# The last feed-forward by seven block products instead of eight, in rounds of three, and the linear attention of the same kernel in another order

## The chip, the cores and the metric

The kernel runs on one core of a Trainium2 chip as a single program. The metric is the time of one execution on the device in microseconds (us). Three executions of the kernel before gave 2459.79, 2460.69 and 2461.81 us; the median is 2460.69 us. One further execution was recorded by the profiler and took 2456.27 us; everything that is read from a trace below is from that one.

The core has a matrix engine (PE, with its weight loads shown apart as PEld), a vector engine (DVE), a scalar engine (ACT), a general engine (POOL) and an engine that mostly issues transfers (SP). Each runs its own queue of instructions in order.

## What is computed

One inference step of a two-layer decoder trunk for 544 tokens: 512 of a prompt and 8 short sequences of 4 tokens. Layer 0 mixes tokens with gated linear attention, layer 1 with a forgetting attention. Before and after each mixer stands a feed-forward, so there are four.

```python
def swiglu(u, w_up, w_down):
    a, b = jnp.split(u @ w_up, 2, axis=-1)
    return (jax.nn.silu(a) * b) @ w_down

def gla_mixer(u, s0, w_in, w_gate2, b_gate, g_out, w_out):
    ...
    q, k, v, r, glr = jnp.split(u @ w_in, [dk, 2 * dk, 2 * dk + dv, 2 * dk + 2 * dv], axis=-1)
    log_a = jax.nn.log_sigmoid((glr @ w_gate2 + b_gate).astype(jnp.float32)) / GLA_TAU
    ...
    o, S = gla_chunk_scan(q * GLA_DK ** -0.5, k, v, log_a, s0)
    o = rmsnorm(o, g_out).reshape(B, L, dv).astype(u.dtype) * jax.nn.silu(r)
    return o @ w_out, S.astype(s0.dtype)

u = modulate(h, P['g_norm'][layer, 2], mod[:, 2, 0], mod[:, 2, 1])
h = h + 0.5 * mod[:, 2, 2][:, None, :] * swiglu(u, P['w_ffn_up'][layer, 1], P['w_ffn_down'][layer, 1])
```

The model width is 1024, the feed-forward's inner width 2816, so `w_up` is 1024 x 5632 (gate columns first, then value columns) and `w_down` 2816 x 1024. The linear attention has 4 heads with keys of 128 and values of 256. Everything is in 32-bit floats.

## The kernel before

**Numbers in two halves.** Every large product is made of three matmuls: an operand x is split into a rounded part (`...h`, written by ACT as a cast) and the rest (`...l`, DVE: x minus the rounded part), and the helper `acc3` adds hi·hi, hi·lo and lo·hi into a PSUM bank (L176 to L178). `halves` (L156) makes the two parts of anything; `split` and `split_cols` (L160, L168) load weights with a transfer and then call it. Weights pass through `raw_tile` (4 buffers), `hi_tile` and `lo_tile` (6 each). PSUM banks for products come from `mm_bank` (5 of them), small ones from `aux_bank` (2).

**Layout.** The 544 columns of tokens stand in two halves of 272, features in 8 blocks of 128 on the partitions (`uh`, `ul` are the input of a feed-forward in two parts, `h` is the residual stream).

**Feed-forward** (`ffn`). The 2816 inner features make 22 pairs of 128 gate and 128 value columns. `up(q, half)` is a gate product `pa` and a value product `pb`, 8 blocks x 3 matmuls each; ACT takes Silu from `pa`, DVE multiplies by `pb` (L446), and `halves` makes `gh`, `gl`. So a pair has 96 up matmuls. `down(qs)` takes a round of pairs (2, then five times 4), loads their rows of `w_down` (128 x 1024 each, one piece) and makes 16 blocks (8 feature blocks x 2 halves) `pd`, each with 3 matmuls per pair of the round. `residual` adds a block into `h`: a DVE operation on the prompt's columns (L393), and in the second half a small DVE product `gs` (L396) and a POOL addition (L398) for the samples. The ups of the next pairs stand behind the 16 blocks of a round. After the last round, `store` transposes `h` and writes the result.

**Linear attention** (`gla`). In order: queries q0 to q3 (`gq`), the third piece of the values with the 16 gate columns (`gv2`), transposes of the gates, then all 8 gate products `z` (L731; contraction over 16 rows), Abs (ACT) and min (DVE) on each; Exp and Ln over all heads (L734, L735), and on DVE per head a subtraction (L737) and a scan (L738), which gives the decay sums `bb`. The other values `gv0`, `gv1` follow (`proj_tokens`), which covers that chain on PE. Then a loop over 4 heads and 7 levels (64 down to 1): DVE (L794) and POOL or DVE (L795) write differences of `bb` to one of four `xb` buffers, ACT takes Exp (L796), DVE and POOL multiply by q and k (L797, L798), PE makes the products of the level (L806), and DVE copies them out (L809, L811). Between the levels `fill` puts projections that don't depend on it on PE: keys k0 to k3 and receptances r0 to r7; the list `FL` says how many after which level. Behind the loop come the samples' part (`ats`, L822 to L842), then per head (L852 to L859) two Exp into a tile `ex`, a product on DVE, a difference on DVE and a product on POOL, which leave q and k ready for the loop over chunks (L899 on), whose transposes `pk` come first.

## Time and profile before

| what | value |
|---|---|
| median of three executions | 2460.69 us (2459.79 to 2461.81) |
| the profiled execution | 2456.27 us |
| its span, first to last instruction | 2454.2 us (2.07 us lie around it) |
| PE busy | 2391.9 us, 97% |
| DVE, ACT, POOL busy | 1236.1, 782.0 and 289.6 us (50, 32 and 12%) |
| mean granted PE clock | 0.986 |
| bytes moved | 319.38 MB, mean 130 GB/s |

A share of the whole span is a mean over stages; the table by stage is shown in the prediction. Matmuls overlap in the records (one of 272 columns lasts 0.29 us while the next starts 0.125 us later), so PE's work is counted by how many start in a full stretch, not by the sum of durations.

### The profile page before, as it was taken

How to read it: one execution, taken by the hardware profiler on the slowest of the kernel's cores; microseconds unless marked ns; L12 is line 12 of the kernel's file. 1: busy time of each engine (PE TensorE's matmuls, PEld its weight loads, DVE VectorE, ACT ScalarE, POOL GpSimd, SP SyncE). 2: the span in 40 equal slices, each digit the busy share in tenths (PEclk: the TensorE clock that was granted, in tenths of full speed). 3: DMA queues.
4: the chain of work that ended last, by engine and by line, in shares of the span. 5: the costliest groups of instructions: out<-in, count | busy, mean ns of one | idle time of the engine just before them, and what ended most of it. 6: DMA issues, size and time to landing. Idle time of an engine off the chain costs nothing.

```text
span 2454.2 us, 48240 instructions
## 1 busy us (share of the span) xinstructions
PE 2391.9 (97%) x20204; PEld 2244.3 (91%) x20204; DVE 1236.1 (50%) x2823; ACT 782.0 (32%) x1430; POOL 289.6 (12%) x448
## 2 busy tenths in 40 slices
PE   8999999999899999999999999999998899999999
PEld 6999999998879999999989999999895589999999
DVE  6343334547666344444584444434848656444433
ACT  4222222334534212222335222222347444222221
POOL 0000000204302010000220000001325120000000
PEclk8999999989999999999999999999999899999999
DMA  9637444313171646445357322322148642222221
GB/s 304 215 115 234 154 167 154 91 48 96 36 223 57 226 141 223 160 167 169 117 152 220 102 86 76 104 87 70 57 104 204 168 125 78 87 92 90 72 84 55
DMA packets 325519, 319.38 MB, mean 130 GB/s; under 512 B 24607, under 2 KB 276349, under 8 KB 325254
## 3 DMA queue, kind: packets, MB, share of 16 engines
q1 hardware_dynamic: 311526, 304.43, 39.0%
q0 software_dynamic: 13776, 11.87, 2.3%
q8 instruction: 159, 2.61, 0.4%
q14 instruction: 58, 0.48, 0.1%
HBM read 298.17 MB, written 18.38 MB: 129 GB/s over the span
## 4 chain that ended last, share of the span: by engine, by line
PE 86%; DVE 5%; DMA 4%; ACT 2%; POOL 1%; issue 1%; SPq 0%; ACTq 0%; DVEq 0%; POOLq 0%
PE pa L176 7%; PE pb L178 7%; PE pb L177 7%; PE pa L177 7%; PE pa L178 7%; PE pb L176 7%; PE pd L176 7%; PE pd L178 7%; PE pd L177 7%; PE ada L231 3%; DMA kd<-khscr 1%; PE kv L588 1%; PE kv L587 1%; PE kv L589 1%; DVE nv L367 1%
## 5 line engine op out<-in xcount | busy, mean ns | idle before, releaser
L176 PE MATMUL pa<-uh,hua 128*128 128x272 f32 x1408 | 410.4, 291 | 1.9 <-ACT uh L386 1.8
L177 PE MATMUL pa<-ul,hua 128*128 128x272 f32 x1408 | 408.6, 290 | 0.4 <-DVE ul L387 0.2
L178 PE MATMUL pb<-uh,lub 128*128 128x272 f32 x1408 | 407.9, 290 | 0.0
L178 PE MATMUL pa<-uh,lua 128*128 128x272 f32 x1408 | 407.6, 289 | 0.0
L176 PE MATMUL pd<-gh,hwd 128*128 128x272 f32 x1408 | 406.8, 289 | 0.0
L176 PE MATMUL pb<-uh,hub 128*128 128x272 f32 x1408 | 406.1, 288 | 0.0
L177 PE MATMUL pb<-ul,hub 128*128 128x272 f32 x1408 | 406.1, 288 | 0.0
L178 PE MATMUL pd<-gh,lwd 128*128 128x272 f32 x1408 | 405.3, 288 | 0.0
L177 PE MATMUL pd<-gl,hwd 128*128 128x272 f32 x1408 | 405.1, 288 | 0.0
L393 DVE SCALAR_TENSOR_TENSOR h<-pd,mods,h 128x272 f32<-128x272 f32 (+1 forms) x384 | 185.2, 483 | 250.8 <-PE pd L178 249.8
L176 PEld LDWEIGHTS pa<-uh,hua 128*128 128x128 f32 x1408 | 266.2, 189 | 14.7 <-issue 6.0
L177 PEld LDWEIGHTS pa<-ul,hua 128*128 128x128 f32 x1408 | 266.4, 189 | 1.6 <-DVE ul L387 1.6
L177 PEld LDWEIGHTS pb<-ul,hub 128*128 128x128 f32 x1408 | 266.7, 189 | 0.0
L176 PEld LDWEIGHTS pd<-gh,hwd 128*128 128x128 f32 x1408 | 265.2, 188 | 1.7 <-issue 1.6
L176 PEld LDWEIGHTS pb<-uh,hub 128*128 128x128 f32 x1408 | 266.4, 189 | 0.0
L178 PEld LDWEIGHTS pb<-uh,lub 128*128 128x128 f32 x1408 | 266.4, 189 | 0.0
L178 PEld LDWEIGHTS pa<-uh,lua 128*128 128x128 f32 x1408 | 266.3, 189 | 0.0
L177 PEld LDWEIGHTS pd<-gl,hwd 128*128 128x128 f32 x1408 | 265.5, 189 | 0.0
L178 PEld LDWEIGHTS pd<-gh,lwd 128*128 128x128 f32 x1408 | 265.4, 188 | 0.0
L446 DVE TENSOR_TENSOR g<-g,pb 128x272 f32<-128x272 f32 x176 | 77.1, 438 | 350.3 <-PE pb L178 348.9
L157 ACT CAST hua<-rua 128x1024 fp32r<-128x1024 f32 x88 | 92.2, 1048 | 461.4 <-PE pd L177 349.6
L398 POOL TENSOR_TENSOR h<-h,gs 128x32 f32<-128x32 f32 x192 | 70.8, 369 | 1237.5 <-DVE gs L396 1232.0
(497 smaller groups left out, 4167.1 us busy)
## 6 DMA issues: line engine op xcount, KB each, us to landing
adaw<-in_w_ada_dram SPq DMA_DIRECT2D x128, 512.0 KB, 6.1
rua<-in_w_ffn_up_dram SPq DMA_DIRECT2D x88, 512.0 KB, 3.8
rub<-in_w_ffn_up_dram SPq DMA_DIRECT2D x88, 512.0 KB, 3.9
rwd<-in_w_ffn_down_dram SPq DMA_DIRECT2D x88, 512.0 KB, 5.0
adah<-in_w_ada_dram SPq DMA_DIRECT2D x16, 512.0 KB, 7.8
adaw<-in_w_ada_kv_dram SPq DMA_DIRECT2D x16, 512.0 KB, 7.5
s<-in_state_gla_dram SPq DMA_DIRECT2D x16, 512.0 KB, 4.2
kp<-in_cache_k_dram SPq DMA_DIRECT2D x16, 512.0 KB, 4.5
```

Of the source, the lines that this page charges most:

```text
L157: S.copy(hi, src)
L176: PE.matmul(ps, lhsT=wh, rhs=xh, start=first and i == 0, stop=False)
L177: PE.matmul(ps, lhsT=wh, rhs=xl, start=False, stop=False)
L178: PE.matmul(ps, lhsT=wl, rhs=xh, start=False, stop=last and i == n - 1)
L231: PE.matmul(ps[32 * j:32 * j + 32, 0:256], lhsT=sc[:, k, :], rhs=t[:, j * 256:(j + 1) * 256], start=k == 0, stop=k == NB - 1)
L367: V.scalar_tensor_tensor(out=v[:, 0:p1 - t0], in0=h[:, k, t0:p1], scalar=mods[:, scale + k, 0:1], in1=rb[:, t0:p1], op0=ALU.mult, op1=ALU. ...
L393: V.scalar_tensor_tensor(out=h[:, m, t0:p1], in0=ps[:, 0:n], scalar=mods[:, gate + m, 0:1], in1=h[:, m, t0:p1], op0=ALU.mult, op1=ALU.add)
L398: G.tensor_tensor(out=h[:, m, TP:T], in0=h[:, m, TP:T], in1=st[:], op=ALU.add)
L446: V.tensor_tensor(out=g[:], in0=g[:], in1=pb[:, 0:HA], op=ALU.mult)
L587: PE.matmul(o, lhsT=xh, rhs=wh, start=k == 0, stop=False)
L588: PE.matmul(o, lhsT=xh, rhs=wl, start=False, stop=False)
L589: PE.matmul(o, lhsT=xl, rhs=wh, start=False, stop=k == NB - 1)
```

## The change

**In the last feed-forward** the call of `ffn` is replaced by a new function `ffn_seven`. Pairs 0 to 2 are computed as before. For the other 19 pairs the up product is regarded as a product of 2 x 2 blocks (gate and value columns by lower and upper 512 rows of the weights, times lower and upper 512 features by the two token halves), and is made with 7 block products, where the plain way has 8. A block product is 4 blocks x 3 matmuls on 272 columns. The sums that this takes: four of the inputs, T1 to T4, once (`inputs`, DVE, 11 operations of 128 x 272 for each of 4 blocks, and `last_input`); four of each pair's weights on POOL (`stage` 0 and 1, 128 x 512 each), whose halves ACT and DVE make in `stage` 1 to 4; and seven per pair with which DVE takes the products out of PSUM (`plus_ps`). The first product goes out by an ACT copy. The lower part `gl` is made by POOL (`low`), in the last round by DVE. Down rounds have 3 pairs (six of them) and 2 (two), and the 16 blocks of a round are put between the 7 products of each pair of the next round (`between`). The rows of `w_down` come as four pieces of 256 columns per round.

**In the linear attention** the projections start as q0, k0, q1, k1, then `gv2`. The gate products `z` stand between the steps of `gv0`; the gate sums of head 0 follow, those of heads 1 to 3 stand behind levels 1, 3 and 5 of head 0 in the loop. q2, q3, k2, k3 join the receptances as fill (a new `FL`), `gv1` moves from before the loop to behind it, and `ex` takes the second `xb` tile in place of one of its own. Weights are loaded by `ahead`, a step or more before their use. The reset pattern `rst` and the gates `gT` move from `kk` heads 0 and 1 to heads 2 and 3.

The whole kernel goes from 18335 to 18107 instructions on PE (228 matmuls fewer), from 2823 to 3082 on DVE, from 1332 to 1431 on ACT, from 448 to 574 on POOL and from 715 to 725 on SP.

```diff
-FL = [i % 2 for i in range(28)]
+FL = [1, 0, 1, 0, 1, 0, 1] + [0, 1, 0, 1, 0, 1, 1] * 3
...
+    def ffn_seven(name, l, s, gate, after_half, steps=(), final=False, plain=3):
...
+        for n in (3, 3, 3, 3, 3, 3, 2, 2):
...
+            def minus(dst, x, y):
+                V.tensor_tensor(out=dst, in0=x, in1=y, op=ALU.subtract)
...
+            def plus(dst, kh, half, k):
+                x, y = block(kh, half, k)
+                V.tensor_tensor(out=dst, in0=x, in1=y, op=ALU.add)
+
+            def inputs():
+                for k in range(H2):
...
+                    plus(x3, 0, 1, k)
+                    plus(x1, 0, 0, k)
+                    minus(x1, x3, x1)
+                    halves(th[1][:, k], tl[1][:, k], x1)
+                    yield
+                    plus(x2, 1, 1, k)
+                    minus(x3, x2, x3)
+                    minus(x2, x2, x1)
+                    halves(th[2][:, k], tl[2][:, k], x2)
...
+                    plus(x4, 1, 0, k)
+                    minus(x4, x4, x2)
+                    halves(th[4][:, k], tl[4][:, k], x4)
+                    yield
+
+            def last_input():
+                S.copy(quarter(uh, 0, 1), t3[:])
+                minus(quarter(ul, 0, 1), t3[:], quarter(uh, 0, 1).bitcast(F32))
...
+            def stage(q, step):
...
+                if step == 0:
+                    o["s3"] = tmp.tile([P, 512], F32, tag="w2", name=f"s3{name}_{q}", bufs=1)
+                    G.tensor_tensor(out=o["s3"][:], in0=a11, in1=a21, op=ALU.subtract)
+                    G.tensor_tensor(out=a21, in0=a21, in1=a22, op=ALU.add)
+                elif step == 1:
+                    t = pair()
+                    halves(t[0][:, 0:2 * W4], t[1][:, 0:2 * W4], ra[:, 0:2 * W4])
...
+                    G.tensor_tensor(out=a11, in0=a21, in1=a11, op=ALU.subtract)
+                    G.tensor_tensor(out=a12, in0=a12, in1=a11, op=ALU.subtract)
+                elif step == 2:
...
+                    halves(t[0][:, W4:2 * W4], t[1][:, W4:2 * W4], o["s3"][:])
+                    halves(t[0][:, 0:W4], t[1][:, 0:W4], a11)
...
+            def product(q, n, w, x):
+                ps = mm_bank(f"p{n}{name}_{q}")
+                acc3(ps[:, 0:HA], [(w[0][:, k], w[1][:, k], x[0][:, k], x[1][:, k]) for k in range(H2)])
+                return ps[:, 0:HA]
...
+            def plus_ps(q, what, ps, x):
+                d = part(q, what)
+                V.tensor_tensor(out=d[:], in0=ps, in1=x[:], op=ALU.add)
+                return d
+
+            def low(q, t0, t1, g):
+                hi, lo = (x[:, t0:t1] for x in gt[q])
+                S.copy(hi, g[:])
+                (G if q not in rounds[-1] else V).tensor_tensor(out=lo, in0=g[:], in1=hi.bitcast(F32), op=ALU.subtract)
+
+            def seven(q, between):
...
+                stage(q + 1, 0)
+                s1 = part(q, "u1")
+                S.copy(s1[:], product(q, 1, o["A11"], B11))
+                between()
+                u2 = plus_ps(q, "u2", product(q, 6, o["S2"], T2), s1)
+                between()
+                a0 = plus_ps(q, "a0", product(q, 2, o["A12"], B21), s1)
+                S.activation(a0[:], a0[:], AF.Silu)
+                stage(q + 1, 1)
+                between()
+                u3 = plus_ps(q, "u3", product(q, 7, o["S3"], T3), u2)
+                stage(q + 1, 2)
+                between()
+                p5 = product(q, 5, o["S1"], T1)
+                c22 = plus_ps(q, "c22", p5, u3)
+                u4 = plus_ps(q, "a4", p5, u2)
+                between()
+                c21 = plus_ps(q, "c21", product(q, 4, o["A22"], T4), u3)
+                V.tensor_tensor(out=c21[:], in0=c21[:], in1=a0[:], op=ALU.mult)
...
+                low(q, t0, t1, c21)
+                stage(q + 1, 3)
+                load(q + 2)
+                between()
+                c12 = plus_ps(q, "c12", product(q, 3, o["S4"], B22), u4)
+                S.activation(c12[:], c12[:], AF.Silu)
+                V.tensor_tensor(out=c12[:], in0=c12[:], in1=c22[:], op=ALU.mult)
+                low(q, t2, t3_, c12)
+                stage(q + 1, 4)
+                between()
...
-            wq = [split_cols(f"gq{i}", W, i * P) for i in range(4)]
...
+            ahead(4)
             for half in range(2):
-                for i in range(4):
-                    feat_block(f"gq{i}", wq[i], half, evac_q(i))
+                for kind, i in wplan[:4]:
+                    feature(kind, i, half)
...
-            proj_tokens("gv", W, vch[:2], evac_v, evac_vs)
...
+            for i in range(3):
+                v0[i]()
+                for _ in range((3, 3, 2)[i]):
+                    gate_half(*zs.pop(0))
+            gate_logs()
+            gate_sums(0)
+            for s_ in v0[3:]:
+                s_()
...
+                    if hd == 0 and li in (1, 3, 5):
+                        gate_sums(li // 2 + 1)
...
+            for s_ in v1:
+                s_()
             ps = aux_bank("ats")
...
-            ex = lo_tile("ex", F32)
+            ex = xb2[1]
...
-    ffn("12", 1, 1, mod(1, 2, 2), store, final=True)
+    ffn_seven("12", 1, 1, mod(1, 2, 2), store, final=True)
```

Where instructions come to stand, at three places. In a row stand the line of its kernel, the operation, the output and the inputs, and the shape. First PE in the linear attention, at the first gate products `z` (`gv0_0`, `gv0_1` are the values' first piece for token blocks 0 and 1). Before:

```order
L723 MATMUL glrT4_5875<-cst_74,glr_5438 16x32
L587 MATMUL gv0_0_5944<-hgv0_1_5932,uh_68 128x352
L731 MATMUL z0_0_5878<-kk_5440,w2_5443 128x272
L731 MATMUL z0_272_5882<-kk_5440,w2_5443 128x272
L588 MATMUL gv0_0_5944<-lgv0_1_5933,uh_68 128x352
L589 MATMUL gv0_0_5944<-hgv0_1_5932,ul_69 128x352
L587 MATMUL gv0_0_5944<-hgv0_1_5932,uh_68 128x352
L588 MATMUL gv0_0_5944<-lgv0_1_5933,uh_68 128x352
L589 MATMUL gv0_0_5944<-hgv0_1_5932,ul_69 128x352
```

And in the changed kernel:

```order
L842 MATMUL gv0_0_5902<-lgv0_3_5899,uh_68 128x352
L843 MATMUL gv0_0_5902<-hgv0_3_5898,ul_69 128x352
L1074 MATMUL z0_0_5928<-kk_5440,w2_5443 128x272
L1074 MATMUL z0_272_5932<-kk_5440,w2_5443 128x272
L841 MATMUL gv0_1_5940<-hgv0_0_5880,uh_68 128x352
L842 MATMUL gv0_1_5940<-lgv0_0_5881,uh_68 128x352
L843 MATMUL gv0_1_5940<-hgv0_0_5880,ul_69 128x352
L841 MATMUL gv0_1_5940<-hgv0_0_5880,uh_68 128x352
L842 MATMUL gv0_1_5940<-lgv0_0_5881,uh_68 128x352
L1074 MATMUL z1_0_5936<-kk_5440,w2_5443 128x272
```

The `z` stood in pairs with five matmuls between two pairs; now the first two stand behind a whole block of `gv0_0`, and the others between the matmuls of the next ones, the fourth 19 matmuls behind the third.

Second, PE behind the attention loop (`at3_0` is the last head's last product, `ats` the samples', `gr4` a receptance, `pk0` the first transposes of the chunks). Before:

```order
L178 MATMUL gr3_1_7337<-uh_68,lgr3_7262 128x272
L817 MATMUL at3_0_7363<-qq_5439,kk_5440 32x32 x16
L838 MATMUL ats_7385<-xb0_6254 32x32 x8
L840 MATMUL ats_7385<-qq_5439,kk_5440 32x32 x4
L176 MATMUL gr4_0_7464<-uh_68,hgr4_7460 128x272
L904 MATMUL pk0_7453<-cst_74,kk_5440 128x128 x4
```

In the changed kernel, the place behind `at3_0`, and the place of `ats`:

```order
L178 MATMUL gr3_1_7177<-uh_68,lgr3_7001 128x272
L1170 MATMUL at3_0_7203<-qq_5439,kk_5440 32x32 x16
L841 MATMUL gv10_0_7249<-hgv10_0_7227,uh_68 128x352
L842 MATMUL gv10_0_7249<-lgv10_0_7228,uh_68 128x352
...
L842 MATMUL gv10_3_7365<-lgv10_3_7246,uh_68 128x352
L843 MATMUL gv10_3_7365<-hgv10_3_7245,ul_69 128x352
L1193 MATMUL ats_7391<-xb0_6088 32x32 x8
L1195 MATMUL ats_7391<-qq_5439,kk_5440 32x32 x4
L1259 MATMUL pk0_7458<-cst_74,kk_5440 128x128 x4
L176 MATMUL gr4_0_7463<-uh_68,hgr4_7150 128x272
```

The second piece of the values, `gv1`, now stands between them: four blocks of 24 matmuls and the samples' own.

Third, DVE at the start of the last feed-forward (`x1`, `x2`, `x4`, `t3` are the sums of inputs, `th`, `tl` their halves; `lu`, `ld` are low halves of weights; `u2` is the first sum that takes a block product out). Before, behind the last `ul` of the second half:

```order
L387 SCALAR_TENSOR_TENSOR ul_69<-nv12_1_7_23200,mods_72,uh_68 128x240
L158 TENSOR_TENSOR gl12_1_23292<-g12_1_0_23343,gh12_1_23291 128x272
L158 TENSOR_TENSOR lua12_3_23585<-rua12_3_23582,hua12_3_23584 128x1024
L446 TENSOR_TENSOR g12_0_1_23398<-g12_0_1_23398,pb12_0_1_23373 128x272
L158 TENSOR_TENSOR lub12_3_23591<-rub12_3_23588,hub12_3_23590 128x1024
L158 TENSOR_TENSOR gl12_0_23223<-g12_0_1_23398,gh12_0_23222 128x272
L158 TENSOR_TENSOR lua12_4_23709<-rua12_4_23706,hua12_4_23708 128x1024
L446 TENSOR_TENSOR g12_1_1_23453<-g12_1_1_23453,pb12_1_1_23428 128x272
```

In the changed kernel at the same place, and where the last of T2 and the first `u2` stand:

```order
L158 TENSOR_TENSOR gl12_1_23243<-g12_1_0_23349,gh12_1_23242 128x272
L534 TENSOR_TENSOR t312_23215<-uh_68,ul_69 128x272
L534 TENSOR_TENSOR x112_0_23409<-uh_68,ul_69 128x272
L534 TENSOR_TENSOR x212_0_23410<-uh_68,ul_69 128x272
...
L158 TENSOR_TENSOR tl212_23213<-x212_3_23659,th212_23210 128x272
L585 TENSOR_TENSOR g12_2_1_23643<-g12_2_1_23643,pb12_2_1_23618 128x272
L527 TENSOR_TENSOR x412_3_23670<-x412_3_23670,x212_3_23659 128x272
L527 TENSOR_TENSOR ul_69<-t312_23215,uh_68 128x4x272
L158 TENSOR_TENSOR gl12_2_23429<-g12_2_1_23643,gh12_2_23428 128x272
L158 TENSOR_TENSOR tl412_23214<-x412_3_23670,th412_23211 128x272
L158 TENSOR_TENSOR ld12_0_1_23744<-rd12_0_1_23741,hd12_0_1_23743 128x768
L643 TENSOR_TENSOR u212_3_23728<-p612_3_23715,u112_3_23700 128x272
```

Where low halves of weights (`lua`, `lub`) and the gated products stood, the 44 operations on inputs stand between them, and `u2` follows behind the last of them.

277 lines of the change are left out of this document (249 added, 28 removed).

## The prediction

> **What bounds the kernel now.** I read the page first, then the table by stretch, the groups of each engine in a stretch, and single rows at the places that the change touches.
>
> ```profile
> PE 2391.9 (97%) x20204; PEld 2244.3 (91%) x20204; DVE 1236.1 (50%) x2823; ACT 782.0 (32%) x1430; POOL 289.6 (12%) x448
> ```
>
> PE is busy 97% of the span. The chain that ended last, by engine:
>
> ```profile
> PE 86%; DVE 5%; DMA 4%; ACT 2%; POOL 1%; issue 1%; SPq 0%; ACTq 0%; DVEq 0%; POOLq 0%
> ```
>
> So matmuls that go away are worth their time wherever PE has no gap, and nowhere else. That is a question to the stretches:
>
> ```profile
> core 0: us, PE busy (x) PEld busy (x) DVE busy (x) ACT busy (x) POOL busy (x), PEclk, DMA share, GB/s
> 524.00:541.00 17.00, 17.00 (x51) 12.62 (x51) 4.69 (x11) 8.31 (x11) 0.00 (x0) 0.60 0.00 1
> 541.00:568.00 27.00, 25.99 (x267) 24.44 (x267) 15.15 (x25) 6.70 (x10) 3.70 (x4) 1.00 0.35 110
> 568.00:640.00 72.00, 65.07 (x1214) 61.72 (x1213) 61.32 (x122) 38.87 (x73) 44.14 (x50) 0.98 0.24 65
> 640.00:656.00 16.00, 12.34 (x120) 11.35 (x119) 7.44 (x16) 9.77 (x16) 4.88 (x11) 0.79 0.16 51
> 2062.00:2084.00 22.00, 22.00 (x177) 22.00 (x177) 9.19 (x13) 8.11 (x13) 0.00 (x0) 1.00 0.31 97
> 2084.00:2420.00 336.00, 336.00 (x2680) 336.00 (x2679) 139.47 (x251) 83.22 (x131) 14.76 (x40) 1.00 0.27 82
> 2200.00:2300.00 100.00, 100.00 (x799) 100.00 (x798) 39.00 (x65) 26.43 (x42) 2.94 (x8) 1.00 0.28 85
> ```
>
> The last feed-forward (2084 to 2420) has PE at 336.00 of 336.00 us, 799 matmuls in 100 us, so 0.125 us for each, and DVE at 39.00 of 100 us. The linear attention's middle (524 to 656) is the other kind: PE idles 6.93 us in 568:640 and 3.66 in 640:656, and the clock is 0.60 in 524:541. There order is worth something, and up to about 23 us in all: at full clock 524:541 would take 17.00 x 0.60 = 10.2, so 6.8 are lost; 1.0 idle in 541:568; 6.9 idle and 1.4 by clock 0.98 in 568:640; 3.7 idle and 3.4 by clock 0.79 in 640:656. Sum 23.2.
>
> **The change part by part. (1) Matmuls.** A pair had 96 up matmuls and has 7 x 12 = 84; 19 x 12 = 228 go, the number by which PE's instructions fall. At 0.125 us in a stretch without gaps: **-28.5 us**. The down matmuls are as many as before.
>
> **(2) DVE in a steady pair.** A pair is now 84 up and 48 down matmuls, 132 x 0.125 = 16.5 us of PE. In that time the other engines have to do more:
>
> ```profile
> L158 DVE TENSOR_TENSOR lub<-rub,hub 128x1024 fp32r<-128x1024 f32 x17 | 20.7, 1220 | 4.2 <-ACT hub L157 4.2
> L393 DVE SCALAR_TENSOR_TENSOR h<-pd,mods,h 128x272 f32<-128x272 f32 x40 | 20.0, 500 | 27.1 <-PE pd L178 27.1
> L158 DVE TENSOR_TENSOR lua<-rua,hua 128x1024 fp32r<-128x1024 f32 x16 | 19.8, 1235 | 26.2 <-ACT hua L157 26.2
> L393 DVE SCALAR_TENSOR_TENSOR h<-pd,mods,h 128x240 f32<-128x240 f32 x40 | 18.7, 466 | 25.6 <-PE pd L178 25.4
> L158 DVE TENSOR_TENSOR gl<-g,gh 128x272 fp32r<-128x272 f32 x38 | 16.7, 439 | 9.2 <-ACT gh L157 9.2
> L446 DVE TENSOR_TENSOR g<-g,pb 128x272 f32<-128x272 f32 x38 | 16.7, 439 | 74.3 <-PE pb L178 74.3
> L396 DVE TENSOR_TENSOR gs<-pd,mods 128x32 f32<-128x32 f32 x40 | 7.2, 181 | 0.0
> ```
>
> A low half of 512 columns and the rows of POOL stand in the groups of the whole run (of ACT's, one row of the stretch 2084 to 2420 ahead of them):
>
> ```profile
> L157 ACT CAST hub<-rub 128x1024 fp32r<-128x1024 f32 x17 | 17.8, 1049 | 16.6 <-PE pb L177 11.6 <-issue 5.0
> ```
>
> ```profile
> L158 DVE TENSOR_TENSOR kx<-hTk,kx 128x512 fp32r<-128x512 f32 x8 | 5.5, 685 | 0.0
> ```
>
> ```profile
> L398 POOL TENSOR_TENSOR h<-h,gs 128x32 f32<-128x32 f32 x192 | 70.8, 369 | 1237.5 <-DVE gs L396 1232.0 <-DVE nrw L151 5.3
> L350 POOL TENSOR_TENSOR sq<-sq,sq 128x272 f32<-128x272 f32 x50 | 42.8, 856 | 95.8 <-ACT sq L346 95.8
> ```
>
> ```profile
> L1404 POOL TENSOR_TENSOR ul<-og,uh 128x512 fp32r<-128x512 f32 x8 | 10.8, 1348 | 49.7 <-ACT uh L1403 49.6
> ```
>
> DVE: seven sums out of PSUM and two products, 9 x 0.439 (row L446) = 3.95; low halves of weights, two of 1024 columns at 1.22 and three of 512 at 0.685 = 4.50; of down weights 4 pieces of 768 per three pairs, 1.33 x 0.92 (three quarters of 1.22) = 1.22; 16 residuals for three pairs, 2.67 x (0.500 + 0.466 + 0.181) = 3.06. Sum 12.7 of 16.5 us, 77%, where it was 39%. POOL: four 128 x 512 sums at 1.348, two lower parts at 0.856, 2.67 additions at 0.369: 8.1 us, 49%. ACT had 26.43 of 100 us, 4.8 in the 18 us of a pair (144 matmuls); its casts of weights grow from three of 1024 columns (3.15 at row `hub`) to the width of 4.5 (4.7), and a copy comes in: about 6.8 us. So all three fit under PE, if they don't hold each other up. DVE and POOL do:
>
> ```profile
> 639.52 1.68 POOL L859 TENSOR_TENSOR kk<-kk,ex 128x512 f32<-128x512 f32 x1 [2.98 <-DVE xb L836]
> ...
> 642.66 1.27 POOL L859 TENSOR_TENSOR kk<-kk,ex 128x512 f32<-128x512 f32 x1 [1.47 <-ACT ex L858]
> 642.69 0.63 ACT L854 ACTIVATE ex<-bb 128x512 f32<-128x512 f32 x1
> 642.71 2.30 DVE L158 TENSOR_TENSOR lgr<-rgr,hgr 128x1024 fp32r<-128x1024 f32 x1
> ```
>
> (start, duration, engine, line and operation). A low half of 1024 columns that takes 1.22 us alone took 2.30 beside a POOL product of 1.27: it grew by 1.08, nearly all of the POOL operation. Of DVE's 12.7 us, 6.6 are operations with both inputs in SBUF like this one (4.50 + 1.22 + 2 x 0.44). If they meet POOL's 49% by chance, 6.6 x 0.49 = 3.2 us are shared; I let DVE bear two thirds, 2.1. That gives 14.8 of 16.5 us, 90%. PE then waits only where a product finds no free bank of the five because DVE came late by more than a few blocks. One pair walked through by these durations has DVE up to 2 us behind and no bank missing. I take 0.15 us per pair, **+3 us**. Bounds: 0, and 12.7 + 8.1 - 16.5 = 4.3 us per pair if every POOL operation stopped DVE for its whole length.
>
> The Trainium skill's page "SBUF — State Buffer", section "Who interferes with whom", says that DVE and GpSimd share a port under an exclusive lock, that a DVE instruction with two SBUF inputs contends with a GpSimd instruction that reads SBUF, and that the one that comes later blocks fully. The pair of rows above agrees. By the rule the loser can be POOL as well, so the sum is between the two bounds and not at one.
>
> ```profile
> rub<-in_w_ffn_up_dram SPq DMA_DIRECT2D x88, 512.0 KB, 3.9
> ```
>
> Transfers: the raw tiles have four buffers, and the weights of two pairs fill them; a piece of down weights between moves the next loads to buffers that come free late. A load takes 3.9 us to land (row `rub`), and its sums are wanted a pair ahead of their products, so I take 0; if DVE stood for it once in each round of three beyond its slack of 1.7 us, 6 x 2.2 = 13 us.
>
> **(3) The start of the last feed-forward.** T2 must be there for the second product of pair 3. DVE can start on it only behind the last input of the second half:
>
> ```profile
> 2061.08 0.83 DVE L387 SCALAR_TENSOR_TENSOR ul<-nv,mods,uh 128x240 fp32r<-128x240 f32 x2
> ```
>
> The inputs end at 2061.9.
>
> ```profile
> 2083.67 0.44 DVE L446 TENSOR_TENSOR g<-g,pb 128x272 f32<-128x272 f32 x1 [0.89 <-PE pb L178]
> ```
>
> This is the multiplication of the sixth half pair, the last plain one of the changed kernel too, so PE's plain part ends near 2083.6 and the first product, which needs only plain inputs, runs to 2085.1. In the order DVE has, from the first input sum to the last T2 half, 54 operations: 48 of 128 x 272, low halves of two 1024, three 512 and one 768. At 0.40 (three operations in 1.22 us at L387 and L367 give that pitch) to 0.44 each: 19.2 to 21.1, plus 2.44 + 2.06 + 0.92 = 5.4: 24.6 to 26.5 us, plus up to 4 us beside four POOL sums of 1.348. So T2 is ready at 2086.5 to 2092, PE waits 1.5 to 7 us, DVE takes the rest of the inputs (about 3 us) ahead of the first sum `u2`, which holds a bank so long, and PE loses some clock. I take **+7**, bounds 1.5 to 12. Before, DVE had 9.19 us of work in 2062:2084, and nothing waited.
>
> **(4) The last two rounds** have two pairs: 16 residuals for two pairs make 4.6 us of DVE per pair for 3.06, and the last round has its lower parts on DVE: **+1** (0 to 4). The blocks of the last round have 6 matmuls, 0.75 us, against 0.466 + 0.181 = 0.65 of DVE, so the tail behind PE's end stays.
>
> Feed-forward: -28.5 + 3 + 7 + 1 = **-17.5 us**.
>
> **(5) Linear attention.** The rows:
>
> ```profile
> L731 PE MATMUL z<-kk,w 16*128 16x272 f32 x16 | 7.1, 584 | 0.0
> ```
>
> of PE in 524:541, of ACT (Ln over all heads; the load of its table) and of DVE in 524:656:
>
> ```profile
> L735 ACT ACTIVATE rr<-rr 128x2176 f32<-128x2176 f32 x1 | 2.0, 2025 | 0.0
> ```
>
> ```profile
> L735 ACT ACT_TABLE_LOAD x1 | 1.3, 1283 | 0.0
> ```
>
> ```profile
> L797 DVE TENSOR_TENSOR xb<-xb,qq 128x256 f32<-128x256 f32 x28 | 18.2, 662 | 5.5 <-ACT xb L796 4.9
> L794 DVE TENSOR_TENSOR xb<-bb 128x256 f32<-128x256 f32 x28 | 16.0, 583 | 0.1
> ```
>
> ```profile
> L738 DVE TENSOR_TENSOR_SCAN bb<-kk,rr 128x544 f32<-128x544 f32 x4 | 4.9, 1273 | 0.0
> ```
>
> ```profile
> L737 DVE TENSOR_TENSOR rr<-rr 128x544 f32<-128x544 f32 x4 | 2.7, 715 | 5.7 <-ACT rr L735 5.7
> ```
>
> The matmuls themselves are the same; what changes is the 23.2 us of losses. *Gate products* (6.8 + 1.0 before): 16 matmul records with 16 rows stand close together at 0.60 clock while PE shows no idle. In the changed order up to 19 full matmuls stand between them, so I take 2.5 in place of 7.8 (0 to 6.8: they may still bring the clock down). *Front*: behind the last `z` stand 48 matmuls of 352 columns and 29 of 272, 48 x 0.161 (0.125 in proportion to columns) + 29 x 0.125 = 11.3 us, against the chain: Exp and Ln 2 x (1.28 + 2.02), subtraction 0.72, scan 1.27, the first level's difference and product, 0.58 + 0.66, and between them an Exp over 512 columns with its table, 1.28 + 0.5 by L735 in proportion to columns: 11.6 us, and Abs of the last `z` ahead of it, another half. So 1.5 lost (0 to 4). *Loop* (8.3 before): heads 1 to 3's sums, 3 x 1.99 us of DVE, now stand inside head 0, between level operations that already run at 0.583 and 0.662 us, above the 0.439 of a wider one alone; the fill is thicker. I take 10 (7 to 15). *Behind the loop* (7.1 before): `gv1`, 96 x 0.161 = 15.5 us, covers the samples' chain and the four `ex` turns, which run one behind the other (two L859 above start 3.14 us apart: 12.6 us), but one of its low halves needs a tile that comes free late: 3 (0 to 7). Sum 17, so **-6 us**, bounds -16 to +10.
>
> The Trainium skill's page "TensorE: Matmul & The Clock Gate", Part 1, ties the half clock to an idle window of about 3.4 us. Here it fell with PE at 17.00 of 17.00 us, so the measurement speaks against it; by the page, spreading `z` would bring nothing, and the -6 would be about -1: 2442 us, a time that the forecast's own case holds already.
>
> **Sum**: -17.5 - 6 = -23.5. On the profiled execution, 2456.3 - 23.5 = 2432.8 us. That execution is 4.4 us under the median of 2460.7, so against the median: **2437 us**.
>
> **The rivals.** *(a) All cover holds*: T inputs cost 1.5 us, the steady pairs nothing, and the linear attention loses 13 of the 23 us. -27 - 10 = -37, so 2424. For it: 39% of DVE and 12% of POOL now. Against it: 24.6 us of DVE in the 22 us that PE gives it. *(c) The linear attention gives back*: gate sums in head 0 and the moved `gv1` cost as in the upper bounds, +10 instead of -6: 2453. For it: ACT and DVE are the chain there, L794 and L797 above their length alone. *(d) DVE becomes the bound of every steady pair*: the lock with POOL stretches its 12.7 us to 18.7, midway between 16.5 and the 20.8 of the upper bound; 2.2 us x 19 = 42 in place of 3, so +15.5 and 2476 us, slower. It decides from about 1.4 us per pair, since 28.5 + 6 - 8 = 26.5 us are there to lose over 19 pairs. For it: the 2.30 us row. Against it: of POOL's 8.1 us per pair, 6 would have to stand in DVE's way. (This is the lock of the Trainium skill's page "SBUF — State Buffer" with DVE always the loser.) *(e) No change*: matmuls go, and PE's time with them turns into bank waits of 1.3 us a pair, 2459; PE's count shows that the change does remove them.
>
> **How the numbers follow.** Forecast 47%, (a) 25%, (c) 12%, (d) 11%, (e) 5%. A measurement of this kernel can tell about 0.2%, 4.9 us, from no change: 2455.8 to 2465.6 is the same. Forecast, (a) and three quarters of (c) are faster: 0.81; (e) and the rest of (c) the same: 0.08; (d) slower: 0.11. The range leaves out (d) and the last part of (a), and takes the bounds of start and loop around the forecast: 2421 to 2463.
>
> **What the profile would show.** 228 matmuls fewer and the steady pairs at 16.5 to 16.8 us with DVE at 80 to 92% (right), or at 18 and more with PE waiting for `u2`, `c22` or `c21` (d). A PE gap of 1.5 to 7 us ahead of pair 3's second product. Low halves `lu` longer than 1.22 and 0.685 where POOL's sums run. A clock above 0.8 around `z`; idle of PE in the loop near 9 us. Wrong would be: PE gaps spread over all pairs; a stage of the linear attention longer than before; time lost in stages that the change doesn't touch.

## The result, and the profile after

The changed kernel takes 2433.0 us in the median of four executions (2429.7 to 2436.4), the kernel before 2460.2 us in the same session. The ratio by which all versions are compared below is 0.9905, with a 95% interval of 0.9887 to 0.9922: 23 us less, between 19 and 28. The two medians lie 27 us apart, near the upper end of that. The profiled execution has a span of 2427.9 us. Its busy times by engine on the page:

```profile
PE 2362.8 (97%) x19976; PEld 2215.4 (91%) x19976; DVE 1381.7 (57%) x3082; ACT 832.4 (34%) x1529; POOL 443.5 (18%) x574
```

PE has 228 matmuls fewer and 29.1 us less of busy time; DVE has 146 us more, POOL 154. The stretches of the changed kernel that answer to those shown of the kernel before, first the linear attention, then the last feed-forward:

```profile
core 0: us, PE busy (x) PEld busy (x) DVE busy (x) ACT busy (x) POOL busy (x), PEclk, DMA share, GB/s
524.00:541.00 17.00, 16.38 (x141) 12.76 (x140) 7.59 (x22) 5.31 (x12) 0.94 (x1) 1.00 0.17 47
541.00:552.00 11.00, 10.39 (x71) 10.17 (x70) 5.77 (x7) 10.09 (x9) 2.33 (x2) 1.00 0.57 169
552.00:632.00 80.00, 69.32 (x1234) 64.19 (x1235) 67.35 (x135) 38.72 (x76) 48.18 (x51) 0.91 0.17 47
632.00:648.00 16.00, 14.96 (x146) 14.11 (x145) 5.98 (x13) 9.53 (x12) 3.66 (x3) 1.00 0.35 99
```

```profile
2080.00:2095.00 15.00, 12.90 (x89) 12.48 (x88) 13.85 (x28) 7.82 (x14) 2.99 (x3) 0.89 0.42 123
2110.00:2160.00 50.00, 50.00 (x400) 50.00 (x399) 42.56 (x71) 20.69 (x35) 26.07 (x27) 1.00 0.32 96
2160.00:2210.00 50.00, 50.00 (x401) 50.00 (x400) 42.55 (x72) 20.77 (x36) 26.23 (x27) 1.00 0.32 96
2310.00:2360.00 50.00, 48.82 (x389) 48.60 (x388) 40.50 (x72) 17.90 (x30) 24.50 (x27) 1.00 0.34 100
```

In the steady pairs PE is busy all the time, 400 matmuls in 50 us, 0.125 us for each as before, with DVE at 85% and POOL at 52%. Just ahead of them, in 2080:2095, PE idles 2.10 us and its clock is 0.89. In the linear attention the stretch around the gate products now has the full clock, and the attention loop (552 to 632) has 10.68 us of idle and a clock of 0.91.

Where the time came from shows when the two changed stages are measured in every trace, each from its first to its last matmul: the linear attention from the first query product `gq` to the last output product `gwo`, the last feed-forward from the last output product `fwo` of the mixer ahead of it to the last transpose `yT`. All times in us:

| trace | linear attention | last feed-forward |
|---|---|---|
| before | 289.5 | 410.1 |
| before, second trace | 292.4 | 408.6 |
| old linear attention, new feed-forward | 289.2 | 388.5 |
| new linear attention, old feed-forward | 285.9 | 411.1 |
| changed | 289.5 | 387.7 |

The feed-forward gives 20 to 23 us in every pairing, 22 in the mean. The stages between these two, which the change doesn't touch, took 1272.9 us in the trace of before, 1269.1 in the changed one and 1269.9 to 1276.1 in the other three; so some 4 of the 26.6 us between the two profiled executions aren't the change's. The linear attention is the same in the two executions first compared, and some 3 us shorter by the mean of all: 290.4 in the three traces of the old order, 287.2 in the five of the new one (289.5, 285.9, and 286.2, 288.9 and 285.7 in three runs below that leave it as changed), though single traces of the two orders overlap. That the first two come out alike is in part the clock, in two places of the stage where it falls in some traces of either order: in the first 10 us and behind the first `gwo`. First the kernel before, then the changed one:

```profile
477.60:487.60 10.00, 9.37 (x79) 9.12 (x76) 7.23 (x25) 3.71 (x8) 0.31 (x1) 1.00 0.28 70
711.20:737.20 26.00, 24.23 (x188) 21.95 (x188) 17.94 (x25) 9.43 (x14) 4.92 (x7) 1.00 0.92 289
```

```profile
477.60:487.60 10.00, 9.37 (x67) 9.15 (x64) 7.15 (x25) 3.39 (x7) 0.24 (x1) 0.83 0.28 70
711.20:737.20 26.00, 24.67 (x188) 22.71 (x189) 15.86 (x23) 8.28 (x13) 5.89 (x7) 0.93 0.85 274
```

The changed one loses up to (1 - 0.83) x 10 + (1 - 0.93) x 26 = 3.5 us there. The second trace of the kernel before has the first loss too, and the trace with the old linear attention and the new feed-forward has both.

### The profile page after: what moved, and what is told of

The parts are those of the page before. It is cut to its first block, busy times and chain, and to the rows that moved or that the text cites. A ratio compares the mean times of both kernels' runs of the same rounds, so it can differ in the third digit from the quotient of the medians.

```text
span 2427.9 us, 48518 instructions
## 1 busy us (share of the span) xinstructions
PE 2362.8 (97%) x19976; PEld 2215.4 (91%) x19976; DVE 1381.7 (57%) x3082; ACT 832.4 (34%) x1529; POOL 443.5 (18%) x574
## 4 chain that ended last, share of the span: by engine, by line
PE 82%; DVE 9%; DMA 4%; ACT 2%; POOL 2%; issue 1%; SPq 0%; ACTq 0%; DVEq 0%; POOLq 0%
PE pd L178 7%; PE pd L176 7%; PE pd L177 7%; PE pa L176 6%; PE pb L178 5%; PE pb L177 5%; PE pa L177 5%; PE pa L178 5%; PE pb L176 5%; PE p L177 3%; PE p L178 3%; PE p L176 3%; PE ada L231 3%; DMA kd<-khscr 2%; DVE nv L367 1%
## 5 line engine op out<-in xcount | busy, mean ns | idle before, releaser
L176 PE MATMUL pa<-uh,hua 128*128 128x272 f32 x1104 | 323.0, 293 | 1.8 <-ACT uh L386 1.7
L177 PE MATMUL pa<-ul,hua 128*128 128x272 f32 x1104 | 321.3, 291 | 0.4 <-DVE ul L387 0.2
L178 PE MATMUL pa<-uh,lua 128*128 128x272 f32 x1104 | 320.0, 290 | 0.0
L178 PE MATMUL pb<-uh,lub 128*128 128x272 f32 x1104 | 319.3, 289 | 0.0
L177 PE MATMUL pb<-ul,hub 128*128 128x272 f32 x1104 | 318.8, 289 | 0.0
L176 PE MATMUL pb<-uh,hub 128*128 128x272 f32 x1104 | 318.3, 288 | 0.0
L178 PE MATMUL pd<-gh,lwd 128*128 128x272 f32 x1056 | 305.1, 289 | 0.0
L176 PE MATMUL pd<-gh,hwd 128*128 128x272 f32 x1056 | 305.0, 289 | 0.0
L177 PE MATMUL pd<-gl,hwd 128*128 128x272 f32 x1056 | 304.8, 289 | 0.0
L178 PEld LDWEIGHTS pd<-gh,lwd 128*128 128x128 f32 x1056 | 199.1, 189 | 0.0
```

The source lines that it names most:

```text
L176: PE.matmul(ps, lhsT=wh, rhs=xh, start=first and i == 0, stop=False)
L177: PE.matmul(ps, lhsT=wh, rhs=xl, start=False, stop=False)
L178: PE.matmul(ps, lhsT=wl, rhs=xh, start=False, stop=last and i == n - 1)
```

## The experiments

All ratios are to the kernel before, timed on the same chip beside it, with their 95% intervals.

**Each half of the change alone.** First `ffn_seven` with the old linear attention:

```diff
-FL = [1, 0, 1, 0, 1, 0, 1] + [0, 1, 0, 1, 0, 1, 1] * 3
+FL = [i % 2 for i in range(28)]
...
     def gla(after_half):
+        ... as before the change
```

> The seven block products alone; the linear attention as before. Theory A (the gain is the feed-forward's, the linear attention nets nothing): 2460 - 24 = 2436 us, range 2433 to 2440, the same as the changed kernel within 4 us. Theory B (the forecast's split: -17.5 feed-forward, -6 linear attention): 2442 to 2443. In the trace the steady pairs run without a PE gap, as in the changed kernel; z again at 0.6 clock.

Measured: 2434.4 us, ratio 0.9908 (0.9888 to 0.9928), as good as the whole change. That is theory A: by the time, theory B's 2442 to 2443 (0.993) lies at the edge of the interval, and the stage in this trace is 20 to 22 us shorter than in the two of the kernel before, not 17.5. One part of the expectation missed: the clock at the gate products. This trace has the old order, and still full clock for most of the stretch:

```profile
524.00:536.00 12.00, 11.77 (x61) 8.79 (x60) 6.93 (x17) 5.45 (x10) 0.00 (x0) 1.00 0.07 26
536.00:540.00 4.00, 4.00 (x15) 3.64 (x14) 1.39 (x3) 3.85 (x4) 0.00 (x0) 0.57 0.00 0
```

Then the new linear attention with the old feed-forward:

```diff
-    ffn_seven("12", 1, 1, mod(1, 2, 2), store, final=True)
+    ffn("12", 1, 1, mod(1, 2, 2), store, final=True)
```

> The new order of the linear attention alone; the last feed-forward as before. Theory A: 2460 +- 3 us, no change: 6.8 us come back around z, and a wait of about 4 us ahead of the first attention product with 5 us at half clock behind it takes them. Theory B: 2454 us. If A, the trace shows the wait for the first POOL product of level 64 again, 3 us or more, with a clock of 0.5 behind it.

Measured: 2455.1 us, ratio 0.9999 (0.9984 to 1.0013). The interval leaves room for 4 us either way and none for the 6 of theory B. The wait at the loop's front is there again, 4.11 us here and 4.12 in the trace of the changed kernel; ACT, DVE and PE of the changed kernel stand around it so (start, duration, operation, idle ahead of it):

```profile
541.65 2.02 ACT L1079 ACTIVATE rr<-rr 128x2176 f32<-128x2176 f32 x1
543.58 1.03 ACT L157 CAST hgq<-rgq 128x1024 fp32r<-128x1024 f32 x1
544.63 1.28 ACT L1080 ACT_TABLE_LOAD   x1
545.92 2.02 ACT L1080 ACTIVATE rr<-rr 128x2176 f32<-128x2176 f32 x1
...
552.49 1.28 ACT L1147 ACT_TABLE_LOAD   x1 [1.36 <-DVE xb L1145]
```

```profile
547.98 1.36 DVE L1083 TENSOR_TENSOR rr<-rr 128x544 f32<-128x544 f32 x2 [2.11 <-ACT rr L1080]
549.26 2.47 DVE L1084 TENSOR_TENSOR_SCAN bb<-kk,rr 128x544 f32<-128x544 f32 x2
551.64 0.77 DVE L1145 TENSOR_TENSOR xb<-bb 128x256 f32<-128x256 f32 x1
```

```profile
555.50 1.11 PE L1157 MATMUL at<-xb 128*64 128x64 f32 x8 [4.12 <-POOL xb L1149]
```

The chain from the last `z` to the first attention product is longer than its own operations: a cast of weights of 1.03 us stands between Exp and Ln, and DVE makes two heads' subtractions and scans (x2 in both rows) where the loop waits for one. PE runs out of work at 551.4 and waits 4.12 us for POOL's product. And the clock falls with it, from about 554.0, where PE still waits, to 560.8:

```profile
551.40:555.50 4.10, 0.00 (x0) 0.00 (x0) 3.62 (x5) 2.20 (x3) 4.00 (x4) 0.82 0.06 15
555.50:561.00 5.50, 5.50 (x69) 4.77 (x69) 4.56 (x10) 1.87 (x3) 3.08 (x4) 0.52 0.30 86
```

**More work between the gates and the loop.** q1 and k1 are needed from the second head on only, so they can cover the chain:

```diff
-            ahead(4)
+            ahead(2)
             for half in range(2):
-                for kind, i in wplan[:4]:
+                for kind, i in wplan[:2]:
                     feature(kind, i, half)
...
             for s_ in v0[3:]:
                 s_()
+            ahead(4)
+            for half in range(2):
+                for kind, i in wplan[2:4]:
+                    feature(kind, i, half)
             ahead(5)
```

> The changed kernel with q1 and k1 (96 matmuls, 12 us) moved from ahead of the values to between gv0 and the attention loop, which needs them only from its second head on. Theory A: the wait at the loop's front (4.1 us, and some 4 us by half clock) goes, PE's cover behind the last z being 19.7 us against a chain of 16: 2433 - 6 = 2427 us, bounds 2424 to 2430. Rival C (the loop is bound by DVE and POOL over its whole length, so a front without a gap only moves the wait into it): within 2 us of the changed kernel, 2431 to 2435, with more idle between 560 and 632.

Measured: 2421.9 us, ratio 0.9860 (0.9838 to 0.9883), 11 us under the changed kernel by the two ratios. The linear attention takes 279.0 us for 287.2. The loop's stretch:

```profile
552.00:632.00 80.00, 75.94 (x1369) 71.47 (x1368) 66.34 (x135) 44.56 (x84) 45.60 (x48) 0.98 0.15 42
```

4.06 us of idle for 10.68 and a clock of 0.98 for 0.91. The first attention product waits for nothing now. One wait of 2.93 us has come in the loop, two levels later, and one of 2.2 us near the start of the stage, ahead of a query product; but the idle as a whole did not move into the loop, so theory A holds and rival C falls. That the whole gain came from the front is not shown: the stage gained 8 us by this trace, where the wait and the clock behind it explain 4.1 and 2.6; the rest of the 11 lies within the intervals.

**gv1 back ahead of the loop.** The other way to cover the chain:

```diff
+            for s_ in v1:
+                s_()
             ahead(5)
...
-            for s_ in v1:
-                s_()
             ps = aux_bank("ats")
```

> The changed kernel with gv1 back ahead of the attention loop, where it covers the gate chain, as before the change. Theory A (gv1's move behind the loop buys the tail and costs the front): the wait ahead of the first attention product goes and the half clock behind it too, -6 to -8 us; behind the loop the chain of the four Exp turns has 15.5 us less cover and the samples' products wait again as in the kernel before, +5 to +8: in all within 3 us of the changed kernel, a ratio of 0.989 to 0.991 to the kernel before. Rival C (the order of z, sums and fill alone gives the gain in the loop, and gv1's place doesn't matter): one of the two waits doesn't show, and the time is 4 us or more off.

Measured: ratio 0.9869 (0.9843 to 0.9896), 283.8 us of linear attention. The ratio lies below the expected 0.989 to 0.991, though its interval reaches into that: the front's wait shrinks to 2.75 us, and the tail waits again, but for less than the front gains.

```profile
541.00:568.00 27.00, 24.10 (x201) 22.88 (x200) 16.01 (x23) 11.89 (x12) 4.31 (x4) 1.00 0.40 122
568.00:640.00 72.00, 65.87 (x1279) 61.86 (x1279) 62.60 (x128) 39.62 (x77) 47.43 (x50) 1.00 0.23 64
640.00:656.00 16.00, 12.72 (x84) 11.29 (x85) 6.64 (x20) 14.77 (x26) 5.04 (x12) 1.00 0.10 34
```

2.90 us of idle ahead of the loop, 6.13 in it, and 3.28 behind it. So by this one trace, 283.8 us against a mean of 287.2, moving `gv1` behind the loop, as the change does, cost about 3 us against leaving it.

**The gate products close together.** All eight `z` behind the first block of `gv0`:

```diff
-                for _ in range((3, 3, 2)[i]):
+                for _ in range((8, 0, 0)[i]):
```

> The changed kernel with all eight gate products behind the first block of gv0, as close together as the two small banks let them be. Theory Z (gate products close together bring the clock down, as the prediction had it): half clock for 5 us or more between the first z and the end of gv0, z at 0.5 us or more in the mean. Rival (the clock there falls in some executions and not in others, for a reason that the order of z doesn't set): full clock, z at 0.39 us, as in the run with the old order and the new feed-forward.

```profile
536.00:542.00 6.00, 6.00 (x25) 4.58 (x24) 2.55 (x6) 3.59 (x7) 0.00 (x0) 0.79 0.00 0
542.00:548.00 6.00, 6.00 (x91) 5.49 (x91) 1.74 (x6) 5.83 (x5) 0.00 (x0) 0.92 0.59 171
```

Half clock for (1 - 0.79) x 6 x 2 + (1 - 0.92) x 6 x 2 = 3.5 us, which costs 1.7, with the `z` themselves at 0.39 us. Neither expectation: the clock does fall, by much less than 5 us. In the one timed execution, 2425.5 us, the linear attention took 281.3 us; the last `z` ran 3 us earlier in its stage, so the gate chain began earlier. One execution is no proof of a gain.

**The kernel before once more**, for a second trace of the same instructions:

> The kernel before, unchanged, for a second trace. Theory Z fixed (the stretch of close z always runs 13 us at half clock): the clock between 524 and 541 is 0.55 to 0.65 again. Rival (the stretch varies from execution to execution): 0.85 or more there, as in the run with the old order and the new feed-forward, and the linear attention is 5 us shorter from its first query to its last output product.

```profile
524.00:541.00 17.00, 16.02 (x52) 11.34 (x52) 6.78 (x17) 7.06 (x12) 0.00 (x0) 0.67 0.00 1
541.00:568.00 27.00, 26.27 (x263) 24.88 (x262) 14.62 (x24) 8.30 (x10) 4.22 (x4) 0.95 0.29 89
```

0.67 between 524 and 541 with 0.95 behind it, near the 0.60 of the first trace, and the linear attention is not shorter but 3 us longer, 292.4. So close `z` lowered the clock in all four traces that have them close, by 1.7 us in two and 6.8 and about 7 in the other two, and spread `z` in none of the eight that have them spread. The direction of the forecast's term holds; its size is not a property of the order.

**The start of the feed-forward.** For pair 3 alone (`plain` is 3), the product with plain inputs goes ahead of the one that needs T2; all others keep their order, behind `else`:

```diff
+                if q == plain:
+                    a0 = plus_ps(q, "a0", product(q, 2, o["A12"], B21), s1)
+                    S.activation(a0[:], a0[:], AF.Silu)
+                    stage(q + 1, 1)
+                    between()
+                    u2 = plus_ps(q, "u2", product(q, 6, o["S2"], T2), s1)
+                    between()
+                else:
...
```

> The changed kernel with the second and third block product of pair 3 in exchanged order: the product with plain inputs comes ahead of the one that needs T2. Theory (the start waits for T2 on DVE): the 2.1 us gap near 2082 becomes 0.6 us or goes, and the clock stays above 0.95 there: -2 us, bounds -3.5 to 0, too little to be sure of by the time, so it is the trace that decides. Rival (DVE is behind with everything, and the first sum out of PSUM is late as well): the gap stays and stands one product later.

Measured: ratio 0.9895 (0.9875 to 0.9915), too little to tell by the time, as expected. The trace: PE's waits there in the changed kernel, and then in this one:

```profile
2084.54 0.40 PE L176 MATMUL p<-th,hu 128*128 128x272 f32 x1 [1.82 <-ACT th L157]
...
2085.21 0.39 PE L177 MATMUL p<-tl,hu 128*128 128x272 f32 x1 [0.27 <-DVE tl L158]
```

```profile
2087.01 0.40 PE L178 MATMUL pd<-gh,ld 128*128 128x272 f32 x1 [1.15 <-DVE ld L158]
```

```profile
2078.70:2098.70 20.00, 18.79 (x148) 18.35 (x147) 19.97 (x41) 9.61 (x17) 5.31 (x5) 1.00 0.31 93
```

T2's wait of 1.82 + 0.27 us is gone, a wait of 1.15 us for the down weights has come, and the clock stays full; the stage takes 384.7 us for 387.7. The theory holds in the main: the start was bound by T2, which DVE makes. The new wait is for DVE too, so the rival's point, that DVE is behind with what follows, is right in part.

**Who holds up DVE.** The weight sums on DVE instead of POOL:

```diff
-                    G.tensor_tensor(out=o["s3"][:], in0=a11, in1=a21, op=ALU.subtract)
-                    G.tensor_tensor(out=a21, in0=a21, in1=a22, op=ALU.add)
+                    V.tensor_tensor(out=o["s3"][:], in0=a11, in1=a21, op=ALU.subtract)
+                    V.tensor_tensor(out=a21, in0=a21, in1=a22, op=ALU.add)
...
-                    G.tensor_tensor(out=a11, in0=a21, in1=a11, op=ALU.subtract)
-                    G.tensor_tensor(out=a12, in0=a12, in1=a11, op=ALU.subtract)
+                    V.tensor_tensor(out=a11, in0=a21, in1=a11, op=ALU.subtract)
+                    V.tensor_tensor(out=a12, in0=a12, in1=a11, op=ALU.subtract)
```

> The changed kernel with the four weight sums of each pair on DVE in place of POOL. Theory L (POOL's sums stretch DVE's two-input operations, and DVE has room left): low halves of 512 columns fall from 1.21 us back to 0.69 and the products L680 from 0.99 to 0.44, about 2.4 us per pair, which pays for four sums of 0.69; DVE stays at 14 to 15 of 16.5 us, PE still waits for nothing in the steady pairs, and the time is that of the changed kernel within 4 us. Rival M (DVE is at its limit, or the longer operations have another cause, such as banks or a slower form): the durations stay, DVE reaches 16.8 us per pair, and 6 to 25 us are lost.

Measured: 2429.8 us, ratio 0.9890 (0.9873 to 0.9908), the same time. DVE's groups in the steady pairs (2110 to 2310), first of the changed kernel, then of this run:

```profile
L158 DVE TENSOR_TENSOR lu<-s,hu 128x512 fp32r<-128x512 f32 x13 | 15.7, 1204 | 1.5 <-ACT hu L157 1.5
...
L680 DVE TENSOR_TENSOR c<-c,c 128x272 f32<-128x272 f32 x12 | 12.8, 1070 | 0.0
...
L672 DVE TENSOR_TENSOR c<-c,a 128x272 f32<-128x272 f32 x12 | 9.8, 816 | 0.4
```

```profile
L158 DVE TENSOR_TENSOR lu<-s,hu 128x512 fp32r<-128x512 f32 x12 | 8.2, 684 | 0.0
...
L680 DVE TENSOR_TENSOR c<-c,c 128x272 f32<-128x272 f32 x12 | 5.4, 450 | 0.0
L672 DVE TENSOR_TENSOR c<-c,a 128x272 f32<-128x272 f32 x12 | 5.3, 440 | 0.3
```

```profile
2160.00:2210.00 50.00, 50.00 (x401) 50.00 (x400) 42.91 (x83) 20.80 (x34) 11.00 (x14) 1.00 0.32 96
```

The low half falls from 1204 to 684 ns, the products from 1070 to 450 and from 816 to 440. DVE does four sums more per pair and is as busy as before, 42.91 of 50 us for 42.55. Theory L: these four sums on POOL cost DVE about what it costs DVE to make them, some 0.7 us each (682 to 832 ns in the means of their four lines in this run). That the two engines meet at all follows the rule of the Trainium skill's page "SBUF — State Buffer", section "Who interferes with whom", on instructions with two SBUF inputs, and the groups agree with it: the sums out of PSUM, with one input there, stay at 0.43 us in both runs. The feed-forward's stage is 384.4 us, as short as with the exchanged product, for two reasons that the trace shows: at the start two waits of 0.79 and 0.90 us with full clock stand for the 2.1 us and the half clock of the changed kernel, and a wait of 1.2 us for POOL near 2336 in the changed kernel is gone.

**More on POOL.** Three further sums per pair, whose result nobody reads:

```diff
                     o["S2"], o["S3"] = view(t, 0), view(t, 1)
+                    G.tensor_tensor(out=o["s3"][:], in0=a11, in1=a12, op=ALU.add)
...
                     o["S1"], o["A22"] = view(t, 0), view(t, 1)
+                    G.tensor_tensor(out=o["s3"][:], in0=a11, in1=a12, op=ALU.add)
...
                     o["S4"] = view(t, 0)
+                    G.tensor_tensor(out=o["s3"][:], in0=a11, in1=a12, op=ALU.add)
```

> The changed kernel with three further sums of 128 x 512 per pair on POOL, whose result nobody reads (4.05 us per pair, POOL at 12 to 13 of 16.5 us). Theory L (what POOL takes from DVE goes with the chance that they meet): DVE's pair grows by about 1.1 us to 15.2, PE still waits for nothing, the same time within 4 us. Rival D of the prediction (each microsecond on POOL is one for DVE): DVE would need 18.1 us per pair, 1.6 x 19 = 30 us slower than the changed kernel, about 2460.

Measured: 2444.2 us, ratio 0.9945 (0.9923 to 0.9968), some 10 us over the changed kernel. Both expectations missed the time; theory L came near for DVE. The stretch of 20 us from 40 us behind the last `fwo` in the changed kernel, then the same stretch and one of steady pairs in this run:

```profile
2076.20:2096.20 20.00, 17.91 (x128) 17.48 (x128) 18.85 (x38) 8.65 (x16) 4.25 (x5) 0.91 0.31 93
```

```profile
2077.60:2097.60 20.00, 15.05 (x98) 14.30 (x97) 18.50 (x34) 7.59 (x15) 4.39 (x4) 0.83 0.30 93
2160.00:2210.00 50.00, 49.48 (x393) 49.07 (x392) 46.04 (x70) 20.00 (x34) 41.13 (x36) 1.00 0.32 94
```

```profile
L675 DVE TENSOR_TENSOR c<-c,a 128x272 f32<-128x272 f32 x12 | 16.9, 1407 | 0.4
```

The product that took 816 ns (L672 of the changed kernel) takes 1407. By the matmuls in the two rows 2160:2210, a pair takes 42.55 x 132 / 401 = 14.0 us of DVE in the changed kernel and 46.04 x 132 / 393 = 15.5 here: three sums on POOL cost 1.5 us, about 0.5 each, where theory L had 1.1 and rival D 4. And PE begins to lose: 393 matmuls in 50 us for 401, some 0.3 us per pair. Whether that is DVE at 92% or POOL, which now stands at 41.13 of 50 us and makes the lower parts `gl`, isn't shown: over 2110 to 2310 the waits of PE and its weight loads that the trace puts down to POOL's `gl` make 1.4 us, those of up products for DVE's `gs` or for a product ahead of them 2.3. The start adds to it: 98 matmuls in the 20 us in which the changed kernel has 128, nearly 4 us. The stage takes 396.5 us for 387.7.

**Both reorderings together**, the front and the exchanged product:

> Both reorderings together (q1 and k1 behind gv0; the plain product first at pair 3). They stand in different stages, so the gains add: the front's 8 to 11 us and the start's 2 to 3, 11 to 13 us under the changed kernel on the same chip, a ratio to the kernel before of 0.985. If they don't add, the ratio is that of the front alone, 0.986 or more, and this run can hardly tell the two apart: the trace decides (no gap of over 1.2 us at pair 3, and none of over 3 us ahead of the first attention product).

Measured: 2424.2 us, ratio 0.9872 (0.9856 to 0.9889). The trace has both gains, 279.5 us of linear attention and 385.0 of feed-forward, against 287.2 and 387.7; by the time this version can't be told from the front alone. Both versions are faster than the kernel before and the changed one, the latter by 0.3 to 0.5% (the interval of the front alone ends below that of the changed kernel; that of this run touches it).

## Why the prediction was right, and where its parts were not

The forecast was -23.5 us and 2437; measured were -23 by the ratio, -27 by the two medians, and 2433. Its two halves were off in opposite directions, 4.5 us too little for the feed-forward and some 3 too much for the linear attention; that the sum fits so well is in that part luck.

**(1) The matmuls**, -28.5: right. PE ran them at 0.125 us, and nothing else became the bound of the steady pairs.

**(2) The steady pairs**, +3: measured 0. The mechanism was right: POOL's sums stretch DVE's operations with two inputs in SBUF, and moving them off showed it. DVE stands at 42.55 of 50 us, 14.0 us per pair for the 14.8 forecast. The term was the mis-sized one: with DVE at 85% and POOL at 52% PE waits for nothing, and only with three further sums on POOL, DVE at 92% and POOL at 82%, does it lose some 0.3 us per pair. Rival (d) would have needed 18.7 us.

**(3) The start**, +7: measured 3.8, right in place and cause. PE waited 2.1 us for T2 (forecast 1.5 to 7), and half clock from about 2086.6 to 2090.0 cost 1.7 more. With the plain product first both go, 1.15 us of another wait come, and the stage gains 3.0.

**(4) The last rounds**, +1: measured 1.2, but not by the way forecast, so its size was luck. The forecast had DVE's residuals and the last round's lower parts; PE waits once, at 2336 where the rounds of two begin, for a lower part made by POOL, and with the weight sums off POOL this wait is gone:

```profile
PE pd L177 <- POOL gl L649: 1.2, 1, 1.2
```

So the feed-forward gave 22 us where 17.5 were forecast; the four terms as measured give -28.5 + 3.8 + 1.2 = -23.5, within 1.5 of it.

**(5) The linear attention**, -6: measured -3 by the traces, 0 with 4 us either way by the time. The stretch behind the front, and the one behind the loop, in the changed kernel:

```profile
561.00:632.00 71.00, 63.82 (x1172) 59.42 (x1167) 59.77 (x122) 34.65 (x70) 41.70 (x43) 0.95 0.17 45
632.00:656.00 24.00, 22.96 (x225) 21.65 (x224) 9.10 (x24) 14.50 (x24) 5.06 (x12) 1.00 0.38 110
```

Counted as the prediction counts, this trace loses 0.6 us at *Gate products* (forecast 2.5), 4.1 by the wait and 5.5 x (1 - 0.52) = 2.6 by clock at *Front* (1.5), 7.2 by idle and 71 x (1 - 0.95) = 3.5 by clock in *Loop* (10), and 1.0 at *Behind the loop* (3): 19 for the 17 forecast, of 23.2 before. The failed step is *Front*. It set 11.6 us of chain and half an Abs against 11.3 of cover and let 1.5 be lost. The cover was right, 11.6 us from the end of the last `z` to 551.4. The chain took 16.1 us, from the start of the last `z` at 539.4 to 555.5, because it was summed from its own operations alone: the weight cast on ACT (1.03) and the second head's subtraction and scan on DVE (about 1.9) stood in the same queues, and the last product was made by POOL (0.96) where DVE's 0.66 had been set. With 12 us more of cover the wait ahead of the first attention product is gone and the stage loses 8 us, which is what shows that this step was the one. The *Gate products* term was right in direction (0.67 and 0.60 to 1.00) and rested on one execution, whose loss of 6.8 us was 1.7 in another trace of the same order. *Loop* came out as forecast. *Behind the loop* was better than forecast where `gv1` stands, but by its one trace `gv1` ahead of the loop was 3 us better for the stage.

## What to carry to other kernels

Matmuls that leave a stretch where PE has no gap are worth their whole time as long as the engines that do the sums instead keep some room: here DVE at 85% of PE's time cost nothing, and DVE at 92% with POOL at 82% a little. Count an operation of POOL as half to the whole of one of DVE where DVE reads two operands from SBUF (0.5 and 0.7 us here, for sums of some 0.7 on DVE). When work is taken out of a chain's cover, sum the chain with everything that stands in the same queues, casts of weights and sums for later heads too. And read a loss by clock in more than one execution before giving a change credit for it.
